# One whole program put under another planner, and two kinds of TensorE work traced behind later projections

## The chip, the cores and the metric

The kernel runs on one core of a Trainium2 chip. The metric is device time in microseconds (us) of one execution. Median of three runs: 1126.58 us, from 1123.9 to 1131.93.

## The reference, cut to what matters

One decoder layer over 512 tokens of width 1024, float32. The first half mixes tokens in two branches, the second half is a squared-ReLU MLP.

- `proj = h @ w_in`, with `h` the modulated RMS norm of `x`. Its columns give r, k, v (1024 each, with a token shift), three low-rank inputs, two halves of a gated convolution input (u1, u2) and two gates (ga, gb).
- RWKV-7 branch, 16 heads of 64: a state per head is carried over 512 steps, `S = S*w_t + (S a_t) b_t + v_t k_t`, `y_t = S r_t`. Then a norm per head (the group norm), `y = norm(y)*gn_gain + gn_bias`, and the **bonus**, `bonus = sum(r*k*r_k) * v` per head, added to it: `y_a = (y + bonus) * g`.
- Convolution branch: a causal depthwise convolution of 31 taps over `u1*sigmoid(u2)`, a layer norm over the channels, SiLU.
- `x = x + gate * (concat(y_a, y_b)*gates @ w_out)`, then the MLP with 4096 hidden columns, then a final RMS norm.

## The kernel before, in words

All matrices are split into a high and a low part, so one projection of 128 columns (`proj`, L458) is 24 matrix products of 128x512 on TensorE: for each of 8 slices of the depth, high by high, low by high, high by low (`mm3`, L165; L174 to L176). Its weights come in two DMAs on SyncE's queue (L159), ScalarE makes the high parts (L150), GpSimd or VectorE the low parts (L151). Its result goes to one of two PSUM banks (tag `pp`).

The RWKV branch works on pairs of heads (8 pairs, j = 0 to 7) and quarters of two pairs (q = 0 to 3). A string, `ORDER`, lists the steps in the order in which they are traced, each with an optional head start in priority (`T1:500`): `Rj` is `rkv_pair`: a small product for the decay (L493), the three projections k, v, r, and `prep_pair` (L505), a chain of VectorE and ScalarE operations that ends in `rt` (L537); the bonus follows it: a product of 128x512 with a block matrix (`pb`, L539, two instructions), a VectorE product with v (`bo`, L541) and a store (L542, SyncE's queue). `Iq` forms chunk products, `Vq` inverts triangular blocks by a chain of 62 small VectorE operations (L598, L600), `Mq` merges the inverses (TensorE, L648), `Oq` prepares operands, `Sq` is the scan over 8 chunks of 64 tokens, `Yq` the group norm (`group_norm`, L706): 16 ScalarE operations (L719), then per pair four transposes on TensorE (`pyt`, L724), a reload of the stored bonus (L726), one VectorE operation (L727) and a store (L729). `Uj` is two projections (u2, u1), `Tj` the 30 convolution taps of a channel tile, each one VectorE operation on 128x512 (`cz`, L745), followed by transposes (`pz`, L750). `Gj` and `Bj` are the gate projections, `W` the output projection, `A` and `L` the modulation of the second half and reloads. The part of `ORDER` that matters here:

```
U1:0v R0 R1:0v I0 U4 R2:0v R3 V0 T1:500 U3 M0 O0 T4 S0:2000 U2:0v I1:100 V1 O1:200 M1 T3:2000 Y0 R4
R5 G0 T2 U6:100 I2 V2:200 G1 S1:500 T6 U7 Y1 R6 M2 O2 R7 T7 I3:1000 V3:1000 U5 S2:100 O3 Y2 U0:100
G2 T5:100 M3 T0 N:1000 B7:2000 B6 S3 B0:100 G5:100 B2 G3 B3 Y3 ...
```

The order in which the instructions of an engine run is fixed when the program is built, by a planner. It plays the program through on a model of the machine, and each time an engine is free there it takes, of the instructions whose inputs and buffers are ready in the model, the one traced earliest (counting the head starts). On the chip each engine then takes its instructions in just that order and waits at each for its inputs. Buffers are single for `rt`, `w1` (shared with `bo`), `yq`, the PSUM tag `y`, and double for the PSUM tag `m` that `pb` uses.

Of the kernel before, what the change touches and what calls it, by code (L numbers as in the profile page):

```python
# [8 lines left out]
F32 = mybir.dt.float32  # L9
# [3 lines left out]
ALU = mybir.AluOpType  # L13
# [5 lines left out]
P = 128  # L19
T = 512  # L20
# [38 lines left out]
EORD = "a0:500 x0:100 d1 s0:200 w0:200 x1:200 x2 a1:500 d2 s1:50 d3 a2 s2:50 m0:50 w1 x3:50 a3:200 m1:100 s3:50 m2:50 m3"  # L59


@with_exitstack
def tile_rwkv7_conformer(
    ctx: ExitStack, tc: tile.TileContext,
    x, c, norm_mix_gain, norm_ffn_gain, ada_w, ada_b, w_in, mu_shift, w0, w_decay_up, a0, w_aaa_up,
    w_gate_up, k_k, k_a, r_k, gn_gain, gn_bias, conv_w, conv_b, conv_ln_gain, conv_ln_bias,
# [2 lines left out]
    nc = tc.nc  # L69
    V, S, G, PE = nc.vector, nc.scalar, nc.gpsimd, nc.tensor  # L70
# [14 lines left out]
    blk1 = const.tile([P, P], F32, name="blk1")  # L85
# [36 lines left out]
    hh = hp.tile([P, KT, T], F32R, name="hh")  # L122
    hl = hp.tile([P, KT, T], F32R, name="hl")
# [39 lines left out]
    def mm3(ps, w, m):  # L163

        for k in range(KT):  # L165
            last = mm3k(ps, w, m, k)
        return last
# [19 lines left out]
    bod = [dram.tile([P, T], F32, name=f"bod{j}") for j in range(KT)]  # L187
# [55 lines left out]
    pq = cq.enter_context(tc.tile_pool(name="pq", bufs=1, space=PSUM, reuse_waits="tile"))  # L243
# [3 lines left out]
    with tc.tile_pool(name="e1", bufs=1) as e1, tc.tile_pool(name="e2", bufs=2) as e2:  # L247
# [11 lines left out]
        def load_ada(j):  # L259
            for s, o in ((1, D), (0, 0)):  # L260
# [19 lines left out]
                        op=ALU.add, axis=AX.X)  # L280
# [35 lines left out]
        for n, _, tag in EARLY:  # L316
            early[n] = (pq if tag == "y" else pp).tile([P, T], F32, tag=tag, name=f"ps_{n}",
                                                       bufs=2 if tag == "pp" else 1)
# [107 lines left out]
        for op in EORD.split():  # L426
            op, hp = (op + ":0").split(":")[:2]
# [25 lines left out]
    with ExitStack() as c1:  # L453
        lp = c1.enter_context(tc.tile_pool(name="lp", bufs=1, reuse_waits="tile"))
        qp = cq.enter_context(tc.tile_pool(name="qp", bufs=1, reuse_waits="tile"))
        tp = tpool[0] = cq.enter_context(tc.tile_pool(name="tp", bufs=1, reuse_waits="tile"))

        def proj(c0, nm):  # L458
            w = wcol(w_in2, c0, nm, lo_eng[0])
            ps = pp.tile([P, T], F32, tag="pp", name=f"ps_{nm}", bufs=2)  # L460
            mm3(ps, w, (hh, hl))
            return ps

        def shift(dst, ps, m):
# [39 lines left out]
        def prep_pair(j, rt, kt, vv, sg, WA):  # L504
            jc = slice(j, j + 1)  # L505

            pl = pq.tile([P, T], F32, tag="m", name=f"pl{j}", bufs=2)
            for tt in range(NT):
                PE.matmul(pl[:, tt * P:(tt + 1) * P], sg[:, tt, :], tri, start=True, stop=True)
            Pt = tp.tile([P, NCHK, 65], F32, tag="Pt", name=f"Pt{j}")  # L510
            Pi = tp.tile([P, NCHK, C], F32, tag="Pi", name=f"Pi{j}")
            G.memset(Pt[:, :, 0:1], 1.0)  # L512
            S.activation(Pt[:, :, 1:65], chunks(pl), AF.Exp, scale=-0.5 * ECON)
            S.activation(Pi, chunks(pl), AF.Exp, scale=0.5 * ECON)

            pa = pq.tile([P, T], F32, tag="m", name=f"pa{j}", bufs=2)
            PE.matmul(pa, WA[64:128, :], lo2[64:128, :], start=True, stop=True)
            at = tp.tile([P, T], F32, tag="sg", name=f"at{j}")
            S.activation(at, pa, AF.Tanh, bias=a0h[:, jc], scale=0.5)

            w1 = tp.tile([P, T], F32, tag="w1", name=f"w1_{j}")
            S.activation(w1, kt, AF.Square, scale=VEC["k_k"][:, jc])
            pn = pq.tile([P, T], F32, tag="m", name=f"pn{j}", bufs=2)
            PE.matmul(pn, blk1, w1, start=True, stop=True)
            S.activation(w1, pn, AF.Ln)
            S.activation(w1, w1, AF.Exp, scale=-0.5)
            V.scalar_tensor_tensor(w1, w1, 1e12, kt, op0=ALU.min, op1=ALU.mult)
            AR = qp.tile([P, NCHK, P], F32, tag="AR", name=f"AR{j}", bufs=4)
            BK = qp.tile([P, NCHK, P], F32, tag="BK", name=f"BK{j}", bufs=BKB)
            V.scalar_tensor_tensor(AR[:, :, 0:C], chunks(w1), kkn[:, jc], Pt[:, :, 0:C], op0=ALU.mult, op1=ALU.mult)  # L530
            V.scalar_tensor_tensor(w1, at, 1.0, w1, op0=ALU.add, op1=ALU.mult)
            V.scalar_tensor_tensor(BK[:, :, 0:C], chunks(w1), kkh[:, jc], Pi, op0=ALU.mult, op1=ALU.mult)
            S.activation(at, at, AF.Identity, scale=kah[:, jc], bias=ka1[:, jc])
            V.tensor_tensor(kt, kt, at, op=ALU.mult)
            V.tensor_tensor(BK[:, :, C:P], chunks(kt), Pi, op=ALU.mult)
            V.tensor_tensor(AR[:, :, C:P], chunks(rt), Pt[:, :, 1:65], op=ALU.mult)
            V.scalar_tensor_tensor(rt, rt, VEC["r_k"][:, jc], kt, op0=ALU.mult, op1=ALU.mult)  # L537
            pb = pq.tile([P, T], F32, tag="m", name=f"pb{j}", bufs=2)
            PE.matmul(pb, blk1, rt, start=True, stop=True)  # L539
            bo = tp.tile([P, T], F32, tag="w1", name=f"bo{j}")  # L540
            V.tensor_tensor(bo, pb, vv, op=ALU.mult)  # L541
            nc.sync.dma_start(out=bod[j], in_=bo)  # L542
            pc = qp.tile([P, NCHK, 1], F32, tag="pc", name=f"pc{j}", bufs=4)
            G.tensor_copy(pc, Pt[:, :, 64:65])
            return dict(AR=AR, BK=BK, v=vv, pc=pc, j=j)
# [161 lines left out]
        def group_norm(q, prs, yq, st):  # L707
            mv = qp.tile([P, NT * 4, 2], F32, tag="mv", name=f"mv{q}")
            rsd = qp.tile([P, NT * 4, 1], F32, tag="rsd", name=f"rsd{q}")
            for tt in range(NT):  # L710
                for h in range(4):
                    V.bn_aggr(mv[:, 4 * tt + h, :], st[:, tt, h:h + 1, :])
            rst = qp.tile([P, NT * 4, 1], F32, tag="rst", name=f"rst{q}")
            V.tensor_scalar(mv[:, :, 1:2], mv[:, :, 1:2], 64e-5, None, op0=ALU.add)
            rsqrt_small(rsd, mv[:, :, 1:2], rst)
            yv = yq.rearrange("p a h n -> p (a h) n")
            V.scalar_tensor_tensor(rst, mv[:, :, 0:1], -1.0, rsd, op0=ALU.mult, op1=ALU.mult)
            for i in range(NT * 4):
                S.activation(yv[:, i, :], yv[:, i, :], AF.Identity, scale=rsd[:, i, :], bias=rst[:, i, :])  # L719
            for pr, d in enumerate(prs):  # L720
                j = d["j"]
                pt = pq.tile([P, NT, P], F32, tag="y", name=f"pyt{q}{pr}")
                for tt in range(NT):
                    PE.transpose(pt[:, tt, :], yq[:, tt, 2 * pr:2 * pr + 2, :].rearrange("p h n -> p (h n)"), ident)  # L724
                yg = tp.tile([P, T], F32, tag="gy", name=f"yg{j}")
                nc.sync.dma_start(out=yg, in_=bod[j])  # L726
                V.scalar_tensor_tensor(yg, pt.rearrange("p a b -> p (a b)"), VEC["gn_gain"][:, j:j + 1], yg,  # L727
                                       op0=ALU.mult, op1=ALU.add)
                nc.sync.dma_start(out=yad[j], in_=yg)  # L729
# [259 lines left out]
        for op in ORDER.split():  # L989
            op, hp = (op + ":0").split(":")[:2]  # L990
# [5 lines left out]
    with tc.tile_pool(name="s3", bufs=2, reuse_waits="tile") as s3:  # L996
# [45 lines left out]
        for fq in range(NFQ):  # L1042
            fh = s3.tile([P, KT, T], F32R, tag="fh", name=f"fh{fq}")
            fl = s3.tile([P, KT, T], F32R, tag="fl", name=f"fl{fq}")
            for i in range(KT):
                if fq == 0 and i < NFF:
                    ps = first_ff[i]
                else:
                    w = wcol(w_ff_in[0], fq * D + i * P, f"fi{fq}{i}", G if fq == 0 and GFI > i else None)
                    ps = pp.tile([P, T], F32, tag="pp", name=f"ps_fi{fq}{i}", bufs=2)  # L1050
                    mm_last = mm3(ps, w, (hh, hl))
                f = s3.tile([P, T], F32, tag="f", name=f"f{fq}{i}")
# [57 lines left out]
```

## Time and profile before

| what | value |
|---|---|
| median of three runs | 1126.58 us |
| the profiled execution | 1131.94 us, span 1130.2 us |
| TensorE (PE) busy | 1023.5 us, 91% of the span |
| VectorE (DVE) busy | 790.1 us, 70% |
| ScalarE (ACT), GpSimd (POOL) busy | 479.1 us, 198.2 us |
| mean granted TensorE clock | 0.953 of full speed |

Busy time of TensorE counts an instruction from its start to a modelled end, so 91% is not 91% of its peak. The stages, by the trace: loads and the first modulation to about 30 us, projections with the RWKV and convolution branches to about 615 us, the output projection to about 770 us, the MLP to the end.

### The profile page before, as it was taken

To read this page: it belongs to the slowest core of one execution; us is meant where nothing else is said; L and a number is where in the kernel's file an instruction comes from. 1 tells how busy PE (TensorE), PEld (TensorE's weight loads), DVE (VectorE), ACT (ScalarE), POOL (GpSimd) and SP (SyncE) were. 2 spreads that over 40 slices of the span, in tenths; PEclk is the share of its full clock that TensorE was granted. 3 is DMA by queue.
4 is the path that set the end of the run, shared out by engine and by line. 5 is a ranking of instruction groups with operands and counts; after the bars stand their busy time and mean duration, and the time that the engine had idled before them with its cause. 6 is when DMAs were issued, how large, how long until landed. Compare 5 with 4: busy or idle time off the path is not lost.

```text
span 1130.2 us, 16757 instructions
## 1 busy us (share of the span) xinstructions
PE 1023.5 (91%) x6037; PEld 792.5 (70%) x6037; DVE 790.1 (70%) x1622; ACT 479.1 (42%) x912; POOL 198.2 (18%) x191
## 2 busy tenths in 40 slices
PE   2999889889899789996997999899999999999995
PEld 1777666656677666665665767688888888888874
DVE  3859999969958997989455787585445445445557
ACT  5546445374644356534343433264323323423432
POOL 1123042222422533221121121200000000000002
PEclk9999999989999989996798999999999999999998
DMA  9622332331343234324257686731223323333332
GB/s 313 181 72 87 88 100 73 54 92 48 104 117 94 86 95 83 85 66 110 94 162 234 224 273 217 232 104 38 84 93 95 101 94 94 95 93 100 96 103 74
DMA packets 184605, 131.34 MB, mean 116 GB/s; under 512 B 49945, under 2 KB 152779, under 8 KB 184523
## 3 DMA queue, kind: packets, MB, share of 16 engines
q1 hardware_dynamic: 184523, 130.28, 39.1%
q8 instruction: 47, 0.77, 0.3%
q14 instruction: 35, 0.29, 0.1%
HBM read 116.61 MB, written 13.63 MB: 115 GB/s over the span
## 4 chain that ended last, share of the span: by engine, by line
PE 43%; DVE 16%; DMA 5%; issue 3%; ACT 3%; POOL 1%; SPq 0%; DVEq 0%; ACTq 0%; POOLq 0%
PE ps_fi L174 5%; PE ps_fi L175 5%; PE ps_fi L176 5%; DVE cz L745 5%; PE acc_fo L1005 4%; PE acc_fo L1004 4%; PE acc_fo L1003 4%; DMA ar<-in_ada_w_dram 2%; DVE tmp L598 1%; DVE aacc L217 1%; PE ps_ga L175 1%; PE ps_ga L176 1%; PE ps_ga L174 1%; DVE X L600 1%; PE pr L669 1%
## 5 line engine op out<-in xcount | busy, mean ns | idle before, releaser
L745 DVE SCALAR_TENSOR_TENSOR cz<-gl,cw,cz 128x512 f32<-128x512 f32 x240 | 200.8, 837 | 3.9 <-ACT cz L743 1.2
L151 DVE TENSOR_TENSOR lo_fo<-raw_fo,hi_fo 128x512 fp32r<-128x512 f32 x64 | 44.2, 691 | 92.1 <-ACT hi_fo L150 91.9
L175 PE MATMUL ps_fi<-hl,hi_fi 128*128 128x512 f32 (+1 forms) x288 | 105.6, 367 | 0.0
L176 PE MATMUL ps_fi<-hh,lo_fi 128*128 128x512 f32 (+1 forms) x288 | 105.3, 367 | 0.0
L174 PE MATMUL ps_fi<-hh,hi_fi 128*128 128x512 f32 (+1 forms) x288 | 105.0, 367 | 0.0
L1003 PE MATMUL acc_fo<-hi_fo,fh 128*128 128x512 f32 x256 | 101.3, 396 | 0.8 <-DVE t_fo L1010 0.8
L1004 PE MATMUL acc_fo<-lo_fo,fh 128*128 128x512 f32 x256 | 101.2, 395 | 0.0
L1005 PE MATMUL acc_fo<-hi_fo,fl 128*128 128x512 f32 x256 | 101.2, 395 | 0.0
L150 ACT CAST hi_fo<-raw_fo 128x512 fp32r<-128x512 f32 x64 | 39.7, 621 | 110.6 <-PE acc_fo L1005 87.8
L151 DVE TENSOR_TENSOR lo_fi<-raw_fi,hi_fi 128x512 fp32r<-128x512 f32 x64 | 43.8, 690 | 52.1 <-ACT hi_fi L150 51.2
L150 ACT CAST hi_fi<-raw_fi 128x512 fp32r<-128x512 f32 x64 | 39.9, 623 | 74.0 <-PE ps_fi L175 45.6
L1021 POOL TENSOR_TENSOR x<-x,fgain 128x512 f32<-128x512 f32 x4 | 5.5, 1392 | 363.8 <-ACT sq L1015 363.8
L175 PEld LDWEIGHTS ps_fi<-hl,hi_fi 128*128 128x128 f32 x288 | 54.3, 189 | 8.9 <-DVE hl L928 0.4
L176 PEld LDWEIGHTS ps_fi<-hh,lo_fi 128*128 128x128 f32 x288 | 54.3, 189 | 8.7
L174 PEld LDWEIGHTS ps_fi<-hh,hi_fi 128*128 128x128 f32 x288 | 54.0, 189 | 8.8 <-ACT hh L927 0.2
L174 PE MATMUL ps_u<-hh,hi_u 128*128 128x512 f32 x128 | 54.1, 422 | 5.4 <-DVE tr L466 2.9
L937 PE MATMUL acc_wo<-lo_wo,mh 128*128 128x512 f32 x128 | 53.0, 414 | 5.9 <-DVE lo_wo L151 3.2
L217 DVE SCALAR_TENSOR_TENSOR aacc<-ar,cact,aacc 128x512 f32<-128x512 f32 x56 | 49.9, 891 | 11.3 <-DMA ar<-in_ada_w_dram 10.7
L1003 PEld LDWEIGHTS acc_fo<-hi_fo,fh 128*128 128x128 f32 x256 | 48.2, 188 | 12.7 <-DVE t_fo L1010 1.3
L1005 PEld LDWEIGHTS acc_fo<-hi_fo,fl 128*128 128x128 f32 x256 | 48.2, 188 | 11.5
L1004 PEld LDWEIGHTS acc_fo<-lo_fo,fh 128*128 128x128 f32 x256 | 48.2, 188 | 11.5
L176 PE MATMUL ps_u<-hh,lo_u 128*128 128x512 f32 x128 | 54.9, 429 | 0.6 <-POOL Pt L512 0.6
(334 smaller groups left out, 2554.3 us busy)
## 6 DMA issues: line engine op xcount, KB each, us to landing
ar<-in_ada_w_dram SPq DMA_DIRECT2D x64, 256.0 KB
raw_fi<-in_w_ff_in_dram SPq DMA_DIRECT2D x64, 256.0 KB
raw_fo<-in_w_ff_out_dram SPq DMA_DIRECT2D x64, 256.0 KB
araw<-in_ada_w_dram SPq DMA_DIRECT2D x8, 1024.0 KB
raw_u<-in_w_in_dram SPq DMA_DIRECT2D x32, 256.0 KB
raw_wo<-in_w_out_dram SPq DMA_DIRECT2D x32, 256.0 KB
raw_k<-in_w_in_dram SPq DMA_DIRECT2D x16, 256.0 KB
raw_v<-in_w_in_dram SPq DMA_DIRECT2D x16, 256.0 KB
```

Of the source, the lines that this page charges most:

```text
L150: S.copy(hi, raw)
L151: (eng or V).tensor_tensor(lo, raw, hi.bitcast(F32), op=ALU.subtract)
L174: PE.matmul(ps[:, ts_], wh[:, i, :], mh[:, k, ts_], start=first, stop=False, skip_group_check=True)
L175: PE.matmul(ps[:, ts_], wh[:, i, :], ml[:, k, ts_], start=False, stop=False, skip_group_check=True)
L176: return PE.matmul(ps[:, ts_], wl[:, i, :], mh[:, k, ts_], start=False, stop=(k == KT - 1), skip_group_check=True)
L217: eng.scalar_tensor_tensor(acc, a, cact[:, k:k + 1], acc, op0=ALU.mult, op1=ALU.add)
L598: V.tensor_tensor(tv, X[:, 0:n, s:s + 1].to_broadcast([P, n, m]), U[:, s:s + 1, s + 1:32].to_broadcast([P, n, m]), op=ALU.mult)
L745: V.scalar_tensor_tensor(cz, gl[:, w:w + T], cw[:, w * KT + j:w * KT + j + 1], cz, op0=ALU.mult, op1=ALU.add)
L937: PE.matmul(wacc[h][tt], mh[k][:, ts_], wl, start=False, stop=False)
L1003: PE.matmul(acc[tt], fh[:, k, ts_], wh, start=(n == 0), stop=False)
L1004: PE.matmul(acc[tt], fh[:, k, ts_], wl, start=False, stop=False)
L1005: PE.matmul(acc[tt], fl[:, k, ts_], wh, start=False, stop=(n == KT - 1))
```

## The change

Two things are changed. The whole body, now called `conformer`, is traced inside one block that asks the planner to play the program through on another, more detailed model of the machine. `ORDER` and every operation stay. And two pieces are no longer traced where they stood: they go to a list, `pending`, with a count, and `proj` runs each when that many more projections have been traced, with an edge that keeps the TensorE instructions of the piece behind the last product of that projection on TensorE's queue (an edge of order alone, no wait). The bonus (L538 to L542) has the count 1, the second half of the group norm (`group_out`, L720 to L729) the count 2 for the first three quarters; the last quarter calls it in place.

```
+def tile_rwkv7_conformer(tc, *args):
+    with tc.block(schedule_with_timeline_sim=True):
+        conformer(tc, *args)
...
+        pending = []
         def proj(c0, nm):
             w = wcol(w_in2, c0, nm, lo_eng[0])
             ps = pp.tile([P, T], F32, tag="pp", name=f"ps_{nm}", bufs=2)
-            mm3(ps, w, (hh, hl))
+            last = mm3(ps, w, (hh, hl))
+            for e in list(pending):
+                e[0] -= 1
+                if e[0] == 0:
+                    pending.remove(e)
+                    with tc.issue_after(last.ins):
+                        e[1]()
             return ps
...
-            pb = pq.tile([P, T], F32, tag="m", name=f"pb{j}", bufs=2)
-            PE.matmul(pb, blk1, rt, start=True, stop=True)
-            bo = tp.tile([P, T], F32, tag="w1", name=f"bo{j}")
-            V.tensor_tensor(bo, pb, vv, op=ALU.mult)
-            nc.sync.dma_start(out=bod[j], in_=bo)
+            def bonus():
+                pb = pq.tile([P, T], F32, tag="m", name=f"pb{j}", bufs=2)
+                PE.matmul(pb, blk1, rt, start=True, stop=True)
+                bo = tp.tile([P, T], F32, tag="w1", name=f"bo{j}")
+                V.tensor_tensor(bo, pb, vv, op=ALU.mult)
+                nc.sync.dma_start(out=bod[j], in_=bo)
+            pending.append([1, bonus])
...
+            if q < 3:
+                pending.append([2, lambda: group_out(q, prs, yq)])
+            else:
+                group_out(q, prs, yq)
+        def group_out(q, prs, yq):
             for pr, d in enumerate(prs):
```

## Rows read from the trace of the kernel before

**Rows 1.** The page: busy us, share of the span and instructions of each engine.
```profile
PE 1023.5 (91%) x6037; PEld 792.5 (70%) x6037; DVE 790.1 (70%) x1622; ACT 479.1 (42%) x912; POOL 198.2 (18%) x191
```
**Rows 2.** Busy time by stretch: length, PE, PEld, DVE, ACT, POOL, clock, DMA, GB/s.
```profile
30.00:770.00 740.00, 666.99 (x4431) 504.06 (x4430) 598.27 (x1261) 342.92 (x675) 182.53 (x165) 0.94 0.42 121
770.00:1070.00 300.00, 300.00 (x1357) 246.28 (x1356) 142.34 (x228) 101.00 (x169) 0.00 (x0) 1.00 0.30 90
120.00:220.00 100.00, 89.70 (x510) 67.53 (x510) 94.44 (x170) 47.11 (x90) 28.29 (x27) 0.94 0.34 82
```
**Rows 3.** What TensorE waited for: us in total, times, longest.
```profile
PE pb L539 <- DVE tr L537: 13.9, 6, 5.0
PE pyt L724 <- ACT yq L719: 12.0, 6, 5.3
PE pz L750 <- DVE cz L745: 7.5, 3, 3.4
```
**Rows 4.** Busy time by stretch again: three stretches at the half clock.
```profile
164.66:171.49 6.83, 6.00 (x16) 4.49 (x17) 5.93 (x18) 1.93 (x4) 1.62 (x3) 0.50 0.34 118
417.25:424.08 6.83, 6.08 (x16) 4.53 (x17) 5.37 (x14) 1.15 (x2) 1.58 (x1) 0.50 0.32 91
519.65:550.37 30.72, 23.82 (x226) 17.17 (x226) 21.62 (x55) 10.94 (x29) 1.27 (x1) 0.50 0.31 87
```
**Rows 5.** TensorE in order of time: start, us, instruction, idle before.
```profile
155.14 0.39 PE L176 MATMUL ps_k<-hh,lo_k 128*128 128x512 f32 x1
...
165.49 2.08 PE L539 MATMUL pb<-tr,blk 128*128 128x512 f32 x2 [4.97 <-DVE tr L537]
...
169.49 0.63 PE L176 MATMUL ps_v<-hh,lo_v 128*128 128x512 f32 x1
...
190.92 1.13 PE L539 MATMUL pb<-tr,blk 128*128 128x512 f32 x2 [2.31 <-DVE tr L537]
...
279.49 0.70 PE L539 MATMUL pb<-tr,blk 128*128 128x512 f32 x1 [1.73 <-DVE tr L537]
...
282.74 0.39 PE L176 MATMUL ps_k<-hh,lo_k 128*128 128x512 f32 x1
...
418.00 2.07 PE L539 MATMUL pb<-tr,blk 128*128 128x512 f32 x2 [4.02 <-DVE tr L537]
...
472.74 0.40 PE L176 MATMUL ps_u<-hh,lo_u 128*128 128x512 f32 x1
...
523.04 0.48 PE L724 MATMUL pyt<-ident,yq 128*128 128x128 f32 x1 [5.34 <-ACT yq L719]
```
**Rows 6.** VectorE's groups from 154.5 to 165.5 us: busy, mean ns.
```profile
L745 DVE SCALAR_TENSOR_TENSOR cz<-gl,cw,cz 128x512 f32<-128x512 f32 x6 | 4.5, 744 | 0.0
L534 DVE TENSOR_TENSOR tk<-tk,at 128x512 f32<-128x512 f32 x1 | 1.7, 1745 | 0.0
```
**Rows 7.** GpSimd in order of time, 152 to 171 us.
```profile
162.12 1.37 POOL L151 TENSOR_TENSOR lo_r<-raw_r,hi_r 128x512 fp32r<-128x512 f32 x1 [0.30 <-ACT hi_r L150]
```
**Rows 8.** VectorE's groups from 470 to 526 us: busy, mean ns.
```profile
L745 DVE SCALAR_TENSOR_TENSOR cz<-gl,cw,cz 128x512 f32<-128x512 f32 x32 | 24.9, 778 | 0.1
L598 DVE TENSOR_TENSOR tmp<-X,U 128x126 f32<-128x126 f32 (+21 forms) x30 | 11.1, 371 | 0.2
L600 DVE TENSOR_TENSOR X<-X,tmp 128x126 f32<-128x126 f32 (+21 forms) x30 | 10.5, 351 | 0.2
```
**Rows 9.** Busy time of the taps (L745) alone: length, DVE, clock, DMA, GB/s.
```profile
510.00:526.00 16.00, 14.33 (x18) 0.80 0.39 60
```
**Rows 10.** The page's costliest group, all 240 taps: busy, mean ns.
```profile
L745 DVE SCALAR_TENSOR_TENSOR cz<-gl,cw,cz 128x512 f32<-128x512 f32 x240 | 200.8, 837 | 3.9 <-ACT cz L743 1.2
```
**Rows 11.** What SyncE's queue waited for at the bonus's store: us, times, longest.
```profile
SPq L542 <- DVE bo L541: 10.8, 3, 9.3
```
**Rows 12.** The first square of a pair (L522): its engine's idle time before it.
```profile
  DMA bod<-bo: 1.3, 1
```
**Rows 13.** GpSimd at the start, in order of time.
```profile
0.80 0.20 POOL L88 MEMSET ident<- 128x128 f32 x1 [0.29 <-POOLq L1097]
```

More of the change, by code (lines that the diff above doesn't have):

```diff
@@ L59, with conformer @@
 EORD = "a0:500 x0:100 d1 s0:200 w0:200 x1:200 x2 a1:500 d2 s1:50 d3 a2 s2:50 m0:50 w1 x3:50 a3:200 m1:100 s3:50 m2:50 m3"
+def tile_rwkv7_conformer(tc, *args):
+    with tc.block(schedule_with_timeline_sim=True):
+        conformer(tc, *args)
 @with_exitstack
-def tile_rwkv7_conformer(
+def conformer(
     ctx: ExitStack, tc: tile.TileContext,
```

## The prediction

> **What bounds the kernel now.** I began with the page's first part: TensorE is busy for 1023.5 of 1130.2 us, VectorE for 790.1 [rows 1]. Then the busy time by stretch, for where the rest lies. From 770 to 1070 us TensorE is busy all 300 us at the full clock: no order can shorten the MLP. From 30 to 770 us it is busy for 667.0 of 740, so 73 us are idle, and the clock granted there is 0.94 on the mean, so 0.06 x 740 = 44 us of work at full speed are lost to it [rows 2]. These 117 us are all that an order can win or lose there. Third, what TensorE waited for: its three longest sums in that stretch are the bonus product for `rt` (13.9 us), the group norm's transposes for ScalarE (12.0) and the taps' transposes for the last tap (7.5), together 33.4 of the 73 [rows 3]. In each the waiting instruction stands at the head of the queue, and projections stand behind it. Fourth, the clock: right after the bonus waits that end at 165.5 and 418.0 us it is 0.50, that is 1.2 GHz for 2.4, for 6.83 us each, and from 519.65 for 30.72 us [rows 4, 5]. A stall is paid a second time, by half of such a stretch.
>
> The waits are of one kind: VectorE is late against what the planner took. In the 11 us ahead of the bonus of pair 2 it did six taps of 0.744 us between the links of the pair's chain, and one link, `tk`, took 1.745 us beside a GpSimd split of 1.37 us [rows 6, 7]; taps and links alone take about 0.74.
>
> **The change part by part.** The sum is made against the profiled execution: 1131.94 us, of which 1.7 lie outside the span. That is 5.4 above the median of the runs shown, which I take off at the end.
>
> *The two deferrals.* What they do depends on where the pieces stand already. I counted the projections (24 products each) in TensorE's order. The bonus of pair 2, for which the count lets pass the projection k of pair 3, stands at 165.49; that k ended at 155.14, and most of v has run as well: the new edge asks for nothing that isn't so [rows 5]. It is the same for pairs 0, 1, 3, 6 and 7. Only pair 4 (at 279.49, its k ends at 282.74) and pair 5 stand ahead of their projection; pair 4 waited 1.73 us, pair 5 not at all [rows 5]. For the transposes it holds in no quarter: those of quarter 2, with the longest wait (5.34 us at 523.04), come 50 us after the second of their two projections ended at 472.74 [rows 5]. So against the old order the edges win 1.7 us, and their value lies in what they forbid the new planner. What moves with them: two TensorE instructions, one VectorE product and one store per pair; four transposes, one reload, one VectorE operation and one store per pair of a quarter. On SyncE's queue the store now comes behind the two weight loads of one more projection. That frees loads which stood behind it (the queue waited 10.8 us at this store in three cases [rows 11]), so I cost it at nothing. From below: the single buffer `w1` is held longer, and the next pair's first square needs it; that wait was 1.3 us, once [rows 12]. Were it so for each of 8 pairs it would be 10 us of ScalarE; products of v and r of that pair cover it. If those have run, it shows.
>
> *The block.* One entry per engine. No row shows one; the nearest is the first instruction at 0.80 us after 0.29 us of idle [rows 13]. I take 0.3 us; up to ten times that for five engines would still be 3, and nothing makes it a gain.
>
> *The order.* The other model re-times everything, and here the trace can give only bounds. Upper: the waits with ready work behind them go. Bonus 13.9, taps' transposes 7.5, group norm's transposes 12.0 less the 5.34 at 523 (below), 6.7: 28.1 us [rows 3, 5], or 38% of the 73. Of the lost clock I leave out the stretch from 519.65 (half of 30.72, 15.4), which leaves 28.6, and take the same 38%: 11. Together 39 us. That ready work was there I checked at the bonus of pair 2: behind it stood the last products of v, done at 169.49, and r, whose last low part was made at 162.12 + 1.37 = 163.5 [rows 5, 7]. Lower: nothing, or a loss (rivals). Between, VectorE decides, for a TensorE that waits less asks more of it. From 120 to 220 us it was idle for 5.6 of 100, while TensorE lost 10.3 idle and 6 to the clock [rows 2]: there a third can be had. Over 30 to 770 it was idle for 142 of 740 [rows 2]: there all. I take half, 20 us, near the stretch where two of the three longest bonus waits stand.
>
> The transposes at 523 I leave as they are. Behind them stand the merge of quarter 3 and its scan, and these wait for the solve of quarter 3 on VectorE, which runs among the last taps [rows 8, 9]. Without the transposes TensorE would wait for those.
>
> All 240 taps took 200.8 us; at 0.744 each they would be 178.6 [rows 6, 10]. These 22 us are VectorE time spent beside GpSimd, as with `tk`. An order that kept them apart could win some of it. The Trainium skill, "SBUF — State Buffer", section "SBUF: two separate sides", says that the port pair that VectorE and GpSimd share is locked for a whole instruction, and the other side is fully blocked if it has two SBUF inputs. By that the 22 us mostly move to another instruction, and the sum stays; without it up to 22 more could go. The row of `tk` agrees with it, no row here tells a moved block from one saved.
>
> Sum: 1131.9 - 20 (order and edges, the 1.7 in it) + 0.3 = 1112.2; less 5.4 for the median, **1107 us**. Its own range by the two bounds, 39 and about 10 us won: 1088 to 1117.
>
> **Rivals.**
> - *The solve of quarter 3 gets free of taps* (better). From 470 to 526 us VectorE did 60 solve operations in 21.6 us and 32 taps in 24.9 [rows 8]. Were the solve ahead of its taps, merge and scan would start some 10 us sooner: the 5.34 us wait and the 15.4 us of clock from 519.65 would go too [rows 4, 5], about 21 us: 1107 - 21 = 1086. For it: the long half-clock stretch has one cause. Against: a chain of small operations leaves gaps that a planner by readiness fills with taps in either model.
> - *The waits only change places*: what TensorE gains ahead it gives back behind VectorE, busy for 94.4 of 100 us from 120 to 220 [rows 2]. 1127, with 1118 to 1136. For it: the three branches share VectorE, and the edges bind in two places of eleven.
> - *The solve of quarter 3 falls behind the taps* (slower). The 18 taps from 510 to 526 us took 14.3 us [rows 9]. If the new model sees them ready first and they run ahead of that chain, merge and scan start 14.3 us later, with TensorE out of projections, since two PSUM banks hold all that may run ahead; half the clock goes with it, another 7. 1127 + 21 = 1148, up to 1160 with a bonus wait and its clock (5 + 3.4 [rows 4, 5]) for one pair more. It decides by how many of those 18 come ahead of the solve's last operation: with 9 or so, the 7 us and their clock eat up half of the 20 won.
> - *It doesn't do what it says*: of the deferrals that is so in 9 of 11 places by the old order, and is in the forecast.
>
> **How the numbers follow.** Chances: forecast 0.42, better 0.13, places only 0.20, slower 0.25. The likeliest gives 1107. For the range I leave out half of the better case and half of the slower one, 0.06 and 0.12: 1080 to 1150. Cases of both signs hold much of the chance; the forecast's own range is 1088 to 1117. A measurement of this kernel can tell 1% from no change, so the bounds are 1115.3 and 1137.8. Faster: 0.42 less a seventh beyond 1115.3 (0.36), 0.13, and a little of the third case: 0.50. Same: 0.06, 0.17 and 0.02 of the slower case: 0.25. Slower: 0.25.
>
> **What would show it.** Right: bonus waits of TensorE under 5 us in sum for 13.9, fewer half-clock stretches between 100 and 440 us, the MLP's 300 us as before, VectorE fuller from 30 to 770 us. The edges: bonus products right behind a projection's last product, with no idle time. The better rival: the solve of quarter 3 in under 30 us and no long half-clock stretch. The slower one: that stretch longer, and the scan of quarter 3 starting later against the taps' end. Wrong altogether if the start (0 to 30 us) or the MLP changes by over 5 us, which I took as fixed, or if one of TensorE's three longest sums is then a wait for weights.

## The result: 7% slower, and the profile after

| | before | after |
|---|---|---|
| median of 4 runs each, same chip | 1129.26 us | 1208.12 us |
| lowest to highest | 1123.9 to 1132.86 | 1205.93 to 1209.32 |
| ratio, with its 95% interval | | 1.0692 [1.0651, 1.0733] |
| the profiled execution, its span | 1131.94, 1130.2 us | 1208.61, 1206.9 us |

The forecast was 1107 us, range 1080 to 1150. The result lies outside it, on the side of a loss.

The page's first part after the change (it answers to [rows 1]), then the busy time by stretch (columns as in [rows 2]; the first two stretches answer to its first two, the first 77 us longer, the second 77 us later; the other four are the longest that ran at half the clock before the end):

```profile
PE 1039.5 (86%) x6037; PEld 820.5 (68%) x6037; DVE 794.0 (66%) x1622; ACT 482.8 (40%) x912; POOL 195.5 (16%) x191
```
```profile
30.00:847.00 817.00, 683.03 (x4415) 529.97 (x4416) 601.73 (x1260) 347.69 (x676) 179.08 (x165) 0.87 0.38 110
847.00:1147.00 300.00, 300.00 (x1366) 247.66 (x1365) 141.78 (x226) 100.69 (x169) 0.00 (x0) 1.00 0.29 90
323.80:347.70 23.90, 19.25 (x210) 14.54 (x208) 21.49 (x52) 8.10 (x17) 4.59 (x5) 0.50 0.10 27
566.10:593.50 27.40, 14.74 (x183) 11.05 (x184) 5.08 (x17) 9.14 (x25) 0.00 (x0) 0.50 0.40 92
634.40:665.10 30.70, 17.05 (x130) 13.33 (x131) 8.53 (x38) 9.63 (x26) 0.00 (x0) 0.50 0.21 69
811.90:835.80 23.90, 10.58 (x45) 9.42 (x46) 18.02 (x69) 12.25 (x33) 0.00 (x0) 0.50 0.19 56
```

The instruction counts are the same, and the MLP still takes its 300 us without a gap. All 77 us lie ahead of it: there TensorE's idle time went from 740 - 667.0 = 73 us to 817 - 683.0 = 134 us (61 more), and its busy time from 667.0 to 683.0 (16 more, for nearly the same instructions at a lower clock). 61 + 16 = 77. VectorE does the same work in a longer time (601.7 of 817 us, before 598.3 of 740): it was not the bound.

What TensorE waited for after the change, from 30 to 847 us (us in total, times, longest; it answers to [rows 3]):

```profile
PE pr L687 <- DVE RV L716: 19.4, 13, 3.4
PE pyt L748 <- ACT yq L737: 14.1, 9, 4.7
PE pmv L228 <- DVE aacc L222: 12.2, 2, 9.8
PE pg L802 <- DMA wg<-in_w_gate_up_dram: 10.8, 2, 9.4
...
PE pb L555 <- DVE tr L551: 2.9, 1, 2.9
```

The bonus (`pb`, 13.9 us before) has all but stopped to wait, as foretold. In its place stand `pr`, the product that opens each chunk of the scan, and `pmv`, the product behind each sum of the second modulation. These are again single waits of a few us, and they don't add up to 61. The milestones show more (start or end of groups of instructions in the two traces, us):

| | before | after | later by |
|---|---|---|---|
| end of the first projection k | 57 | 69 | 12 |
| end of the solve of quarter 0 | 202 | 236 | 34 |
| start, end of scan 0 | 227, 266 | 264, 335 | 37, 69 |
| end of scan 3 | 577 | 647 | 70 |
| output projection, first and last product | 616, 753 | 687, 807 | 71, 55 |
| first product of the MLP | 753 | 831 | 78 |

Four places lose time: the start (12), the solve of quarter 0 (66.8 us for 47.5), scan 0 (71 us for 39), and the 24 us between the output projection's last product and the MLP's first (none before). Between scan 0's end and the MLP some is won and lost again: scan 1 takes 33 us more, but the solves of quarters 1 and 2 take 41 and 33 us for 64 and 65, with 11 and 6 taps among their links for 28 and 37. So the new order isn't the worse one at every chain.

**How the start looks.** From 30 us to the end of the first projection k, before and after (columns as in [rows 2]):

```profile
30.00:57.10 27.10, 26.78 (x137) 21.53 (x136) 24.19 (x54) 14.36 (x28) 3.85 (x4) 1.00 0.60 174
```
```profile
30.00:69.20 39.20, 33.50 (x132) 26.79 (x133) 24.73 (x60) 15.52 (x30) 3.59 (x7) 0.78 0.46 133
```

Of the 12 us, 5.4 are idle time of TensorE (0.3 before, 5.7 after), and 6.7 are more busy time for nearly the same instructions, at a granted clock of 0.78 for 1.00.

**How the scan looks.** TensorE in order of time in scan 1, one chunk, before and then after the change (start, us, instruction; rows of other products between left out):

```profile
335.02 0.68 PE L669 MATMUL pr<-RV,M 128*64 128x64 f32 x8
335.62 0.71 PE L184 MATMUL pA<-AR,BK 64*128 64x128 f32 x6
336.26 0.27 PE L184 MATMUL psa<-Rs,RT 64*64 64x64 f32 x1
...
337.44 0.40 PE L176 MATMUL ps_ga<-hh,lo_ga 128*128 128x512 f32 x1
337.77 0.27 PE L691 MATMUL pn<-RV,BT 128*64 128x64 f32 x1
```
```profile
382.94 0.68 PE L687 MATMUL pr<-RV,M 128*64 128x64 f32 x8
383.55 0.50 PE L179 MATMUL ps_v<-hh,hi_v 128*128 128x512 f32 x1
...
386.50 0.94 PE L189 MATMUL pA<-AR,BK 64*128 64x128 f32 x12
387.37 0.27 PE L189 MATMUL psa<-Rs,RT 64*64 64x64 f32 x1
...
391.25 0.39 PE L179 MATMUL ps_r<-hh,hi_r 128*128 128x512 f32 x1
...
392.93 0.27 PE L709 MATMUL pn<-RV,BT 128*64 128x64 f32 x1
```

The chain is `pr`, a copy on ScalarE, `psa`, a copy, `pn`, an addition on VectorE, the next `pr`. Before, `pn` came 2.75 us after `pr`, with three projection products between. After, 12 products of `ps_v` run between `pr` and `psa` and 19 of `ps_v` and `ps_r` ahead of `pn`: 10 us. ScalarE's copy behind `pr` had been done at 384.47 (start 384.10, 0.37 us), 2.9 us before its user's turn came. TensorE is never idle in this stretch, so no view of waits shows it. In the trace up to 620 us the mean unbroken run of projection products is 8.3 before and 15.3 after. Scan 1, from its first `pr` to its last, took 90 and 123 us. Of the 90, 60 are its first chunk, with 157 projection products between `pr` and `psa`; from the second chunk on it took 29 and 100 us. Scans 2 and 3 then have chunks with no projection left between them, and in scan 3 and just behind it TensorE stands idle at half the clock (the stretches from 566.1 and 634.4).

**How the solve looks.** The taps on VectorE during the solve of quarter 0 up to its last two links, before and after (length of the stretch, busy time of the taps alone, clock, DMA share, GB/s):

```profile
154.60:200.50 45.90, 6.62 (x10) 0.89 0.25 76
```
```profile
169.50:235.30 65.80, 27.01 (x30) 0.95 0.26 78
```

20 more taps stand among the 62 links of the solve, 20.4 us, and the solve takes 19.3 us longer. VectorE is busy for 42.8 and 62.1 us of the two stretches, so there was no room to hide them. It is the case of my slower rival, in quarter 0, not in quarter 3.

**How the wait ahead of the MLP looks.** TensorE from the last product of the output projection to the MLP's first (idle time before, and its releaser, in brackets):

```profile
807.44 0.39 PE L962 MATMUL acc_wo<-hi_wo,ml 128*128 128x512 f32 x1
817.63 1.84 PE L228 MATMUL pmv<-ones,aacc 128*128 128x1 f32 x8 [9.80 <-DVE aacc L222]
822.81 1.94 PE L942 MATMUL ph<-ident,xn 128*128 128x128 f32 x8 [3.34 <-DVE srow L140]
825.59 2.16 PE L942 MATMUL ph<-ident,xn 128*128 128x128 f32 x8 [0.84 <-DVE hf L949]
831.16 1.22 PE L179 MATMUL ps_fi<-hh,hi_fi 128*128 128x256 f32 x4 [3.41 <-ACT hh L951]
```

The eighth sum of the modulation and its product `pmv` come after all 384 products of the output projection; before, 331 of them stood ahead of it and 53 covered the row norms that need it. Now nothing does. But its place on TensorE is not what makes `pmv` late: it starts as soon as VectorE has ended the sum. VectorE after the change, in order of time:

```profile
791.58 2.58 DVE L222 SCALAR_TENSOR_TENSOR aacc<-ar,cact,aacc 128x512 f32<-128x512 f32 x2 [1.67 <-DMA ar<-in_ada_w_dram]
...
800.19 0.69 DVE L156 TENSOR_TENSOR lo_fi<-raw_fi,hi_fi 128x512 fp32r<-128x512 f32 x1 [2.57 <-ACT hi_fi L155]
...
803.87 0.48 DVE L220 TENSOR_SCALAR aacc<-ar,cact 128x512 f32<-128x512 f32 x1
...
816.74 0.74 DVE L222 SCALAR_TENSOR_TENSOR aacc<-ar,cact,aacc 128x512 f32<-128x512 f32 x1
```

The seventh sum ends at 794, and the eighth begins only at 804, behind low parts of MLP weights for which VectorE waits. Before, the two were 2.6 us apart (719.8 and 722.4), and the eighth ended at 735.

### The profile page after: what moved, and what is told of

Same layout as the page of the kernel before. It is cut to its first block, busy times and chain, and to the rows that moved or that the text cites. A ratio compares the mean times of both kernels' runs of the same rounds, so it can differ in the third digit from the quotient of the medians.

```text
span 1206.9 us, 16773 instructions
## 1 busy us (share of the span) xinstructions
PE 1039.5 (86%) x6037; PEld 820.5 (68%) x6037; DVE 794.0 (66%) x1622; ACT 482.8 (40%) x912; POOL 195.5 (16%) x191
## 5 line engine op out<-in xcount | busy, mean ns | idle before, releaser
L769 DVE SCALAR_TENSOR_TENSOR cz<-gl,cw,cz 128x512 f32<-128x512 f32 x240 | 202.5, 844 | 4.5 <-issue 1.4
L1027 PE MATMUL acc_fo<-hi_fo,fh 128*128 128x512 f32 x256 | 93.6, 397 | 1.1 <-DVE t_fo L1034 1.1
L180 PE MATMUL ps_u<-hl,hi_u 128*128 128x512 f32 x128 | 53.5, 418 | 0.0
```

The costliest lines, as they stand in the source:

```text
L180: PE.matmul(ps[:, ts_], wh[:, i, :], ml[:, k, ts_], start=False, stop=False, skip_group_check=True)
L769: V.scalar_tensor_tensor(cz, gl[:, w:w + T], cw[:, w * KT + j:w * KT + j + 1], cz, op0=ALU.mult, op1=ALU.add)
L1027: PE.matmul(acc[tt], fh[:, k, ts_], wh, start=(n == 0), stop=False)
```

## The experiments

Each median is of 4 to 10 runs, beside 7 to 13 runs of the kernel before on the same chip; ratios are to these, and are not the quotients of the two medians. "The changed kernel" is the one with the whole change.

**1. The parts apart.** My first theory, A, blamed the deferrals (late bonus, and `w1` held longer); B blamed the new order.

Deferrals alone, the old model:
```
-    with tc.block(schedule_with_timeline_sim=True):
-        conformer(tc, *args)
+    conformer(tc, *args)
```


> The two deferrals under the old planner, without the new model. Theory A (the deferred bonus is at fault: its store is late, holds the single buffer w1, and the next pair's first square waits for it; that square of pair 2 came at 170.9 us after the change for 136.0 before): slower, 1165 to 1210 us. Rival B (the order of the new model is at fault, whatever the deferrals do): 1120 to 1140 us, as before.

Measured: 1136.33 us, 1.0069 [1.0035, 1.0104].

The new model alone, no deferrals:
```
 def tile_rwkv7_conformer(tc, *args):
+    with tc.block(schedule_with_timeline_sim=True):
+        conformer(tc, *args)
```


> The new model alone, the bonus and the group norm's second half traced where they stood before. Theory A: 1110 to 1145 us, the square of pair 2 at about 136 us again. Rival B: 1185 to 1210 us, near the changed kernel, scan 0 ending at about 335 us.

Measured: 1237.42 us, 1.0992 [1.0935, 1.1049].

The changed kernel with the bonus back in its place, the group norm still deferred:
```
-            pending.append([1, bonus])
+            bonus()
```


> The changed kernel with the bonus called in place; the group norm's second half stays deferred and the new model stays. Theory A: 1115 to 1150 us. Rival B: 1185 to 1210 us. If it lies near the new model alone, the deferred group norm costs nothing.

Measured: 1237.83 us, 1.0984 [1.0918, 1.105].

The changed kernel with a buffer of its own for `bo`:
```
-                bo = tp.tile([P, T], F32, tag="w1", name=f"bo{j}")
+                bo = tp.tile([P, T], F32, tag="bo", name=f"bo{j}")
```


> The changed kernel with one thing more: the bonus's result gets a buffer of its own, so that the next pair's first square no longer waits for its store. Theory A, if w1 is the gate: at least half of the 79 us back, 1130 to 1170 us. If the late bonus hurts by other means (its banks of PSUM, the scan): 1170 to 1205. Rival B: 1200 to 1212 us, no change.

Measured: 1209.54 us, 1.0744 [1.0687, 1.08].

What follows: A falls. The deferrals cost 0.7% under the old model, and under the new one the bonus's wins 30 us (1237.8 to 1208.1); the group norm's does nothing with the bonus in its old place (1237.4 and 1237.8), nor does the buffer. The new model's order costs about 109 us, and the deferral gives 30 back. The wait for the bonus with the new model alone and, second, with the bonus back:

```profile
PE pb L544 <- DVE tr L542: 15.9, 4, 12.4
```
```profile
PE pb L555 <- DVE tr L551: 22.6, 5, 12.8
```

One bonus product held TensorE for 12 us there, with the new model alone up to 256.5 us, ahead of scan 0. Scan 0 then started at 288 us, for 264 in the changed kernel.

**2. Long runs by another way, priorities, and the place.** Theory C: whole projections between the scan's small steps are the cost.

The old model, with every projection's products pulled ahead:
```
-            mm3(ps, w, (hh, hl))
+            with ahead(700):
+                mm3(ps, w, (hh, hl))
```


> The old planner and no deferral, but every projection's 24 products get a head start of 700 in priority: in the finished order TensorE's mean unbroken run of projection products is then about 14, as in the changed kernel, for 8 in the kernel before. Theory C (long unbroken runs put the small chain products of the solves and scans behind whole projections; that alone costs the time): slower than before, 1160 to 1240 us, with scans of the first two quarters 25 us longer or more and more stretches at half the clock late. Rival D (run length is only a mark; the loss lies in what the new model does on VectorE and ScalarE or in its buffers): 1120 to 1140 us.

Measured: 1294.49 us, 1.1457 [1.1408, 1.1506]. Runs nearly as long as those after (13.6 products on the mean) cost 165 us under the old model too, more than I had said. But the scans took 40, 105, 39 and 96 us (first `pr` to last), for 39, 90, 51 and 66 before, not 25 us more in the first two: here the first solve started at 243 us for 155. That long runs can cost so much is shown, that the scans are where is not.

The changed kernel with the scans at a head start of 2000:
```
-... S1:500 ... S2:100 ... S3 ...
+... S1:2000 ... S2:2000 ... S3:2000 ...
```


> The changed kernel with the head starts of the scans of quarters 1 to 3 raised to 2000 (500, 100 and none before). In the finished order the mean run of projection products stays at 14. Theory C (the new model finds the scan's next product not ready when it is ready on the chip, so that no priority pulls it ahead): 1195 to 1220 us, scan of quarter 1 still over 110 us. Rival E (the head starts were tuned for the other model, and the scans only lack priority): under 1180 us, scan of quarter 1 under 100 us.

Measured: 1212.95 us, 1.0719 [1.0668, 1.0771]; scan 1 took 124 us. E falls: these head starts don't mend the chain.

The new model for the stage of the branches and the output projection alone, and the same cut with the old model:
```
     with ExitStack() as c1:
+        with tc.block(schedule_with_timeline_sim=True):    # control: tc.block()
...
```


> No deferral; only the stage with the two branches and the projections (from about 20 us to the last gate) is planned with the new model, the start and the MLP with the old one. Theory C: the loss of the new model without deferrals (1237 us) sits in this stage, all but about 12 us of the start: 1190 to 1240 us. Rival F (the whole program as one plan is what costs, or the start): under 1160 us.

> The same cut of the program into stages as in the run with the new model in the mixing stage alone, but all planned with the old one: what the cut itself costs. All theories: 1130 to 1150 us, some us above before, since work of one stage can't run ahead into the other in the plan.

Measured: 1234.34 us, 1.0937 [1.0879, 1.0994], and 1130.19 us, 0.9993 [0.9962, 1.0024]. Nearly all of the new model's loss arises in that stage, and the cut is free.

**3. The scans relieved by hand.** Edges of order alone hold later projections behind the scan's three steps of each chunk:
```
+        def gated(ps, w):
+            for k in range(KT):
+                g = gates.pop(0) if gates else None
+                with tc.issue_after(g) if g is not None else nullcontext():
+                    last = mm3k(ps, w, (hh, hl), k)
+            return last
...
+                gates.append(g0.ins)        # after pr; likewise after psa and pn
```


> The changed kernel, with edges of order alone that spread three projections traced after a scan over its 8 chunks: three products behind each of the chunk's three steps on TensorE (9 a chunk). Nothing pulls the scan's own steps ahead. In the finished order 9 to 21 projection products then stand between two chunks of scans 0, 2 and 3, for 0 to 72. Theory C (scans stretched by whole projections between their steps are where most of the time went): scans 0 and 2 take 45 to 60 us for 73 and 80, and the time falls to 1150 to 1190 us. Rival G (the scans are late for another reason, such as their inputs or VectorE, or the time saved there is lost again before the next quarter): scans 0 and 2 shorter or not, 1195 to 1225 us.

> The same edges and deferrals under the old planner. Theory C: its order had 3 to 12 projection products between most chunks already, so the edges bind in few places: 1125 to 1150 us. Were the edges a gain in themselves, under 1118 us; then what they do under the new model says less about it.

Measured: 1204.03 us, 1.0703 [1.065, 1.0755], and under the old model 1174.93 us, 1.044 [1.0399, 1.0481]. Scans 0 and 2 took 47 and 50 us, as C said, and the time hardly moved. The second run shows one reason: the edges cost the old order 39 us, and the projection k of pair 4, which starts at 218 us with the deferrals alone, now waited for the scan (266). So I left the first two projections after each scan free:
```
             yq = qp.tile([P, NT, 4, C], F32, tag="yq", name=f"yq{q}")
+            gates[:] = [None] * 16
```


> As the run with edges from the scans' steps to three later projections, but the first two projections traced after each scan are left free, for those edges held back the projections that TensorE had run ahead of scan 0 under either planner (they cost the old planner's order 39 us too: 1175 for 1136). Under the new model 9 to 21 projection products then stand between most chunks, for 0 to 72. Theory C (unbroken runs of projections between the scans' steps cost about 40 of the 78 us; the rest is the start, 12, and the wait ahead of the MLP, 23): 1160 to 1185 us. Rival G (the scans' lengths matter little; with the same edges the two planners' orders lie 72 us apart again): 1195 us or more.

> The same later edges under the old planner. Its order between the chunks hardly changes (2 to 18 projection products), so both theories expect 1130 to 1145 us, near the deferrals alone (1136); the time of the run under the new model is to be read against this one.

Measured: 1196.03 us, 1.0591 [1.0525, 1.0657], and 1134.51 us, 1.0066 [1.0036, 1.0095]. The edges are now free under the old model, and under the new one they win 12 us, not the 40 of theory C. C falls in its size, and 1196 us is in G's range (the two planners' orders then lie 62 us apart, for 72). Scan 0 still started at 261 us, so the lateness ahead of it was to be looked for.

**4. The solve relieved by hand.** Theory H: on every engine the new order puts ready bulk between the links of serial chains, and each place has its price. (The shorter solves of quarters 1 and 2 speak against it on VectorE.)
```
             for w in range(1, CW):
+                with tc.issue_after(solved[0]) if j == 3 else nullcontext():
                     V.scalar_tensor_tensor(cz, gl[:, w:w + T], ...
```


> The changed kernel with one set of edges of order alone: the 30 taps of channel tile 3 stay behind the last operation of the solve of quarter 0 on VectorE. In the finished order 6 taps then stand among that solve's operations, for 30 (9 in the kernel before). Theory H (the new order hands VectorE ready taps between the links of the solve, as it hands TensorE ready projections between the links of the scan; 21 taps too many are some 16 us, and the first scan sets what follows): the solve of quarter 0 takes about 48 us for 66, scan 0 starts 12 to 18 us sooner, and the time is 1188 to 1200 us. Rival I (the taps held back come back as lateness elsewhere, the first scan's start doesn't set the end): 1203 to 1215 us.

> Both sets of edges under the new model: the taps of channel tile 3 behind the solve of quarter 0, and the later projections spread over the scans (1196 us without the taps' edges). Theory H: the two add up, 1175 to 1188 us. Rival I: 1193 us or more.

Measured: 1200.13 us, 1.0649 [1.0599, 1.0699], and with both sets of edges 1174.42 us, 1.0413 [1.0366, 1.0459]. With the taps' edges the stretch that answers to the two above holds

```profile
170.00:208.00 38.00, 6.61 (x7) 1.00 0.30 89
```

and scan 0 starts at 246 us for 264, 18 sooner. Alone that is worth 8 us, just outside the range that I gave H. Added to the scans' edges it is worth 22 (1196.0 to 1174.4): the two together win 34, more than 12 + 8, so each place hid part of the other. TensorE with both (columns as in [rows 2]):

```profile
30.00:815.00 785.00, 677.79 (x4419) 516.31 (x4419) 588.31 (x1259) 346.07 (x674) 179.88 (x165) 0.90 0.40 114
```

Idle 107 us for 134. That is 34 of the 72 us by which the new order is worse than the old one with the same deferrals (1208.1 to 1136.3). The scans' edges are free under the old model; the taps' edges were not run under it.

**5. The start and the end.** The new model for the branches alone; start, output projection and MLP under the old:
```
+        first = steps.index("W:2000")
+        with tc.block(schedule_with_timeline_sim=True):    # control: tc.block()
...
+            for op in steps[:first]: ...
+        for op in steps[first:]: ...
```


> The change as it is, deferrals included, but the new model plans only the stage of the projections and the two branches (to the last step ahead of the first output projection); the start, the output projection and the MLP are planned by the old model. Theory H: the start's 12 us and the 23.7 us ahead of the MLP (the sums of the second modulation stand behind other ready work) go, the rest stays: 1168 to 1190 us. Rival J (the wait ahead of the MLP is only the branch stage's lateness handed on, and comes with either planner): 1195 us or more.

> The same cut into stages and the deferrals, all under the old model: both theories 1128 to 1142 us, near the deferrals alone (1136).

Measured: 1213.94 us, 1.0758 [1.0702, 1.0814], and 1168.78 us, 1.0356 [1.0318, 1.0395].

The control missed what I expected, and the first run lies in J's range, but for a cause that neither theory held: the cut costs 32 us by itself (1168.8 for 1136.3), because the sums of the second modulation can't start ahead of it. TensorE's wait for them, with the new model for the branches and then in the control:

```profile
PE pmv L227 <- DVE aacc L221: 33.6, 2, 31.9
```
```profile
PE pmv L227 <- DVE aacc L221: 32.7, 2, 31.0
```

Against its own control the new model loses 45 us, for 72 where it plans everything. So, if the cut costs the same in both, 45 arise in the branches, and 27 where it also plans the start and the end. The first projection k ended at 56 us, and the MLP's first product came 1 us after the output projection's last: with those stages planned by the old model neither the 12 us nor the 24 are there, late as the branches are. So J falls in its reason.

Both sets of edges and a third, on SyncE's queue (the later weights too get an edge, behind the last load of the list):
```
+                with tc.issue_after(head_dma[0]) if g else nullcontext():
                     d = nc.sync.dma_start(out=raw, in_=wv[g, :, :, c0:c0 + P]).ins
```


> The last run with both sets of edges (1174 us) and a third: on SyncE's queue the second halves of the first four weights, and the weights of later projections behind them, stay behind the last load of the first modulation, as in the kernel before. Theory H (at the start too, ready bulk, here weight loads, was put ahead of the chain that the projections wait for): the first projection k ends at 57 to 61 us for 68, and the time is 1160 to 1168 us. Rival L (the start's 12 us are made up later, VectorE sets the pace of the branches): 1171 us or more.

Measured: 1180.55 us, 1.0458 [1.0423, 1.0494], no better than the 1174.4 without. The first projection k still ended at 68 us. H falls here: the order of these loads is not what makes the start longer. The time is what L said, but L's reason (the 12 us are made up later) was not tested, since the start got no shorter. Five of the eight modulation loads went out ahead of the weights anyway, and the last three waited for a free buffer until 31 us.

The same with all eight sums at a head start of 3000:
```
-... A3:200 W A0 W:100 ... A5:2000 ... A7:200 A1:1000 ... A6 ... A2 W A4 ...
+... A3:3000 W A0:3000 W:100 ... A5:3000 ... A7:3000 A1:3000 ... A6:3000 ... A2:3000 W A4:3000 ...
```


> As the run with three sets of edges, with the head starts of the second modulation's eight sums all at 3000. In the finished order VectorE's other operations between a sum and its result fall from 31 to 2, but on TensorE the last sum's product still stands behind all 384 products of the output projection, as in the changed kernel (331 in the kernel before). Theory H (what counts is that TensorE's product stands behind ready bulk): the wait ahead of the MLP stays over 15 us, and the time within 8 us of the run without. Rival K (the sums only lack priority): the wait under 8 us, and the time 10 us or more below it.

Measured: 1175.83 us, 1.0433 [1.0396, 1.047]. The wait ahead of the MLP is 20 us (777 to 797), for 24 without, so K falls, and both numbers are in H's range. But H's reason, the place of `pmv` behind all 384 products, is not what the trace shows. VectorE's last operation of the eighth sum, and TensorE:

```profile
782.56 0.75 DVE L223 SCALAR_TENSOR_TENSOR aacc<-ar,cact,aacc 128x512 f32<-128x512 f32 x1
```
```profile
783.45 1.84 PE L229 MATMUL pmv<-ones,aacc 128*128 128x1 f32 x8 [5.91 <-DVE aacc L223]
```

`pmv` starts 0.1 us after its sum has ended. What is late is the sum on VectorE: its eight operations took from 767 to 783 us, among low parts of MLP weights and the additions behind the output projection. An earlier `pmv` alone would have waited for it. In the run with the old model for the start and the end the eighth sum ended at 819 us, 20 us ahead of the output projection's last product, and there was no wait; no run brought it that far forward under the new model.

No version beat the kernel before.

## Why the prediction was wrong, point by point

- **What bounds the kernel.** Right in where: the MLP is untouched (300.00 of 300), all of the change lies ahead of it. One term does not carry over. I counted 44 us of lost clock from the mean granted clock and added it to the idle time. By the same count the stretch from 30 to 847 us would have lost 0.13 x 817 = 106 us, 62 more, but TensorE's busy time rose by 16 only. At half the clock stood 96 us before and 208 after, and TensorE was busy for 84 and 144 of them: of the 112 us more, 52 were idle anyway, and are counted twice. In the trace of before only 12 of 96 were, so the 44 are little off there.
- **The two deferrals.** That they do next to nothing against the old order held: 1.0069, a loss of 7 us where I had a gain of 1.7. That "their value lies in what they forbid the new planner" held too, and was larger than thought: 30 us. In five of eight pairs the bonus stands right behind a projection's last product, in four of them with no idle time, as I said it would:

```profile
117.96 0.40 PE L181 MATMUL ps_u<-hh,lo_u 128*128 128x512 f32 x1
118.19 1.02 PE L555 MATMUL pb<-tr,blk 128*128 128x512 f32 x2
```

- **Costed at nothing.** SyncE's queue waited 27.2 us at the bonus's store, once 24.0, for 10.8 before [rows 11]. The wait of a pair's first square for the store rose from 1.3 to 7.9 us of ScalarE, below my bound of 10. The buffer of its own for `bo` leaves the time where it was (1209.5 and 1208.1), so nothing was hung on `w1`.

```profile
SPq L558 <- DVE bo L557: 27.2, 4, 24.0
```

- **The block.** The first weight load is issued at 0.81 us, for 0.80 before; the control of the cut at the branches is at 0.9993. Nothing, as costed.
- **The order: the step that failed.** I took 20 us of gain, "near the stretch where two of the three longest bonus waits stand", between 39 and "nothing, or a loss (rivals)". The upper bound came from rows; the lower one I left to a single rival of 21 us in one place. I took the waits for what the other model would win. It does not win them: with the new model alone the bonus waits for 15.9 us, for 13.9 before, and only with the deferral for 2.9 (the deferral under the old model: 14.1); the group norm's transposes wait for 14.1 us, for 12.0. And the waits were the visible part of an order that served the chains well. In place of a gain of 20 us the new order costs 109 without the deferrals and 72 with them. The trace of before could not have given that number: no row of it shows the other model. But it bounds it: past the first, a chunk of scan 1 took 4 to 6 us there with 3 to 12 projection products between, and each of the 28 steps from chunk to chunk, the links of four solves and the eight modulation sums is a place where a whole projection (24 products at 0.23 us, 5.5 us) or a run of taps can stand. A loss of several times 21 us was open by that count.
- **Start and MLP taken as fixed.** The MLP yes. The start only up to 30 us: the first product of a projection comes at 32.7 us for 30.9, and the 12 us arise from there to 69 us. The 24 us ahead of the MLP I had not taken apart from it. So none of my signs of "wrong altogether" came: the one wait for weights near the top, `pg`, is the fourth sum. And three signs of "right" came in a kernel 7% slower: bonus waits of 2.9 us, 7 stretches at half the clock from 100 to 440 us for 9 (but 61 us of them for 41), the MLP's 300 us. Only VectorE, 553.5 of 740 us for 598.3, said no. Signs taken from the waits could not tell.
- **The rivals.** "The solve of quarter 3 falls behind the taps": right mechanism, wrong quarter, and too small. In quarter 0 20 more taps cost 20 us, and the edges that take them out give 18 back at scan 0's start. The solve of quarter 3 itself took 37.3 us for 40.4. "The waits only change places" is true of the names in the list, not of the sum: idle time rose by 61 us. The chain falls behind where TensorE is busy (scan 1), and the idle time comes later, where no projection is left.
- **The 22 us of the taps.** All 240 took 202.5 us, for 200.8 [rows 10]:

```profile
L769 DVE SCALAR_TENSOR_TENSOR cz<-gl,cw,cz 128x512 f32<-128x512 f32 x240 | 202.5, 844 | 4.5 <-issue 1.4
```

  With nearly every instruction at another time, the sum hardly moved; in the 20 kernels of this case it lies between 198.5 and 207.9 us, and none wins the 22. The Trainium skill, "SBUF — State Buffer", section "SBUF: two separate sides", has the port pair of VectorE and GpSimd locked for a whole instruction; I had taken it that such time moves and is not saved. The sums agree with that. How much of the 22 us is time beside GpSimd no run here shows.

What is shown: the new model's order does it, in the stage of the branches above all (45 of 72 us by the pair of cuts); edges against the taps inside the first solve and the projections inside the scans win back 34 of the 72; more priority mends neither the scans nor the sums. What stays open: why the new model's start is 12 us longer (the load queue's order was not it), the rest inside the branches, and why the new model finds the chain's steps later than the old one does. That it lets an engine take ready work far ahead, so that the next link isn't ready in the model when its turn comes, would fit the scans' and the sums' indifference to priority; no run here looked into the model itself.

## What to carry to other kernels

A hand-tuned order is tuned against the planner that plays it out: put the same program under another model and every place where a serial chain shares an engine with ready bulk is decided anew, so bound the loss by the number of such places, not by one. Look for chains that are late without any idle time: the distance from one link to the next (here `pr` to `pn`, 2.75 and 10 us) shows what sums of waits hide. Two sets of edges of order at the right links gave back 34 us, while edges in the wrong place cost 39, and a control under the old planner is what told the two apart.

## What the runs showed of the hardware that was not expected

TensorE's clock fell to 1.2 GHz (granted 0.50) also where TensorE was busy for 19.25 of 23.9 us (323.8 to 347.7); in the 6.8 us ahead, at the full clock, it had been busy for 5.2. No row here explains it. Where it was idle for more than half of the time (811.9 to 835.8: busy 10.58 of 23.90) the half clock still made the groups of small products on the chain to the MLP twice as long: `pmv` x8 took 1.84 us and `ph` x8 1.94. At the full clock, before the change, they took

```profile
737.87 0.95 PE L223 MATMUL pmv<-ones,aacc 128*128 128x1 f32 x8
...
745.63 1.03 PE L918 MATMUL ph<-ident,xn 128*128 128x128 f32 x8
```

With one `pmv` and two `ph` groups ahead of the MLP's first product that is, by my estimate, some 3 us of the 24. In all, TensorE's busy time grew by 16 us for nearly the same instructions.
